# A decoder layer: the recurrence's values and gates projected in pieces of 264, 264 and 512 tokens in place of 264, 264, 256 and 256

## The chip, the core and the metric

The kernel runs on one core of a Trainium2 chip. The metric is the device time of one execution in microseconds (us); the median of several executions is given. The engines are PE (TensorE's matmuls, with PEld its weight loads), DVE (VectorE), ACT (ScalarE), POOL (GpSimd) and SP (SyncE, which here only issues transfers). Each runs its own instructions in order and waits for the others by semaphores. [...]

## The reference

One layer on 16 meta tokens and 1024 tokens of width 1024: a SwiGLU half step, a mixing block of two parallel groups of heads (a gated linear recurrence, HGRN2, with 4 heads of 128, and stick-breaking attention with 8 heads of 64), and a second SwiGLU half step.

```python
h = h + 0.5 * swiglu(rms_norm(h, ffn1_norm[l]), ffn1_w_in[l], ffn1_w_out[l])
u = rms_norm(h, mix_norm[l]) @ w_in[l]
hq, hf, hi, hg, sq, sk, sv = jnp.split(u, ..., axis=-1)
o_hg = hgrn2(hq, hf, hi, hg, lb_all[l], hgrn_out_norm[l], valid)
o_sb = stick_breaking(sq, sk, sv, sb_q_norm[l], sb_k_norm[l], valid)
h = h + jnp.concatenate([o_hg, o_sb], axis=-1) @ w_out[l]
h = h + 0.5 * swiglu(rms_norm(h, ffn2_norm[l]), ffn2_w_in[l], ffn2_w_out[l])
```

In the recurrence, `hf` gives the gate `f = lb + (1 - lb) sigmoid(hf)` and the key `k = (1 - lb) sigmoid(-hf)`, `hi` is the value `v`, `hq` the query and `hg` the gate of the output. Values and keys are needed for all 1040 tokens, queries and output gates for the 1024 behind the meta tokens.

## The kernel before

Activations are kept with the model's width on the partitions and the tokens along the free dimension. Each fp32 operand is split into a high and a low part, and `product` (L250) makes a product from three matmuls per block of 128 rows: high by high (L257), low weights by high (L258), high weights by low (L259). A projected column block (128 columns of `w_in` for n tokens) is therefore 8 x 3 = 24 matmuls of n tokens into one PSUM bank.

The stages, in order of time: the first SwiGLU (to about 690 us in the profile), the attention's projections, then three stages in which the order of PE's instructions is written out by the program:

- **The weave** (`weave`, L1735, over `tasks`, L2164) projects the attention's q, k and v for four pairs of heads (`sb_project`, L1375) while other engines turn and normalise them. At its end it takes the first steps of `hgrn_fill` (L1126): v and f of the recurrence's head 0.
- **The braid** (`braid`, L1705) lays the stick-breaking attention, job by job (score pieces `z`, transposes `flip`, products `oacc`), between further steps of `hgrn_fill`. It sums the planned time of the attention's steps, multiplies it by 1.22, and takes steps of projection from `columns` until that much planned time is covered. What it takes in one round is spread evenly over the round.
- **The rest** (`rest`, L2211) runs the steps of `columns` that are left, while the recurrence's heads (`hgrn_attend`, L1193) load their data back from DRAM and begin; then a second weave runs the recurrence (`lvl`, `km`, `knp`, `s`, `up`, `op`, `onp`) between the steps of the output projection's attention half (`wo`, `mix_out`, L1677). The second SwiGLU follows at about 1325 us.

`hgrn_fill` goes through the heads' columns in the order v, f, q, g. Each column is cut into pieces of tokens: q and g by HALVES (512 and 512), v and f by PIECES. Each piece is two steps of 12 matmuls, and each step carries its planned time, `12 * (n * 0.42 + 13)` ns. Behind the second step of a piece, `use` reads the bank: for v one copy on ACT (L1143), for f two sigmoids on ACT (L1149, L1150) and two operations on DVE (L1151, L1154), for q and g one sigmoid on ACT (L1157) and a product on DVE that reads the bank again (L1158). The results go through buffers `st` to DRAM (`hg_v`, `hg_k`, `hg_f`, `hg_q`, `hg_g`). The tokens from 528 on are written in reverse order, which the recurrence uses.

In the weave the projections take turns between two banks; in the braid one of the two holds a column of zeros for the scans (`idle`), and all pieces use the other (`proj_bank`, L1097, `proj_tags`). The weights of a column are loaded and split ahead of it (`col_tile`, `split_w`: L240 casts the high part on ACT, L242 makes the low part on DVE).

PE's order is the program's. On ACT, DVE, POOL and SP the framework arranges the instructions, so their order can change with PE's.

Of the kernel before, what the change touches and what calls it, by code (L numbers as in the profile page):

```python
# [27 lines left out]
EPS = 1e-6  # L28
HALVES = [(META, 512), (META + 512, 512)]
CHUNKS = [(META + 512, 512), (0, 264), (264, 264)]  # L30
PIECES = [(0, 264), (264, 264), (528, 256), (784, 256)]
LEVELS = [1, 2, 4, 8, 16, 32, 64]
NEG = -1e30

# [15 lines left out]
class Block:  # L50
# [1075 lines left out]
    def hgrn_fill(self, xh, xl, pool, dst):  # L1126
# [56 lines left out]
        for i, (kind, _) in enumerate(plan):  # L1183
            for ci, (c0, n) in enumerate(PIECES if kind in "vf" else HALVES):
                for half in range(2):
# [599 lines left out]
    def run(self):  # L1785
# [21 lines left out]
        with ExitStack() as c0:  # L1807
            with ExitStack() as c1:
# [352 lines left out]
                columns = self.hgrn_fill(xh, xl, pst, hgD)  # L2161
                oH, self.att = [], []

                def tasks():  # L2164
                    done = []
                    for i in range(4):
                        for x in done[i - 2] if i > 1 else ():
                            yield "join", x
                        done.append(
                            (yield from self.sb_project(i, xh, xl, mixb, mix, (qD, kD, vD)))  # L2170
                        )
                        if i == 2:
                            next(jobs)
                    for t, f in islice(columns, 16):
                        f()
                        yield t

                with tc.manual_schedule(engines={nc.tensor.engine}):
                    cf = ExitStack()
                    fetch = self.pool("fetch", ctx=cf, side="right")  # L2180
                    jobs = self.sb_jobs((qD, kD, vD, oD), fetch, self.att)
                    with ExitStack() as c2:
                        mixb = self.pool("mixb", ctx=c2)
                        mix = self.pool("mix", ctx=c2)
                        self.weave(tasks())
                    with ExitStack() as c2:
                        self.att.append(self.pool("att1", ctx=c2))
                        tag = self.proj_tags[0]
                        self.proj_tags = [self.proj_tags[1]] * 2
                        self.idle = self.pproj.tile([P, 1], F32, tag=tag, name="idle", bufs=1)  # L2190
                        nc.vector.memset(self.idle, 0.0)
                        self.braid(jobs, islice(columns, 76), 1.22, 2.0, 3.0)
                    cf.close()
                    self.proj_tags[0] = tag
                    hg_ctx = ExitStack()
                    hg = self.pool("hg", ctx=hg_ctx, side="right")
                    heads = [self.hgrn_attend(h, hg, hgD, oH) for h in range(4)]
                    self.wide = hg.tile([P, 5, 512], U8, name="wide")
                    for i, n in enumerate(LEVELS[:5]):
                        m = self.masks[:, i, :].rearrange("p (b h r) -> p b h r", h=2, r=n)  # L2200
                        wide = self.wide[:, i].rearrange("p (h c x) -> p h c x", h=2, c=4)
                        for half in range(2):
                            for c in range(4):
                                nc.vector.tensor_copy(
                                    wide[:, half, c].rearrange("p (b r) -> p b r", r=n),
                                    m[:, :, 1 - half, :],
                                )
                    for h in range(3):
                        next(heads[h])

                    def rest():  # L2211
                        left = list(columns)
                        for t, f in left[:-1]:
                            f()
                            yield t
                        left[-1][1]()

                    self.weave(rest(), heads[:3], 1e6, 1.0, True)
# [183 lines left out]
```

## Time and profile before

| | us |
|---|---|
| median of 3 runs | 1961.46 |
| lowest, highest | 1961.43, 1961.83 |
| the profiled execution: its time | 1963.76 |
| the profiled execution: its span | 1962.1 |

The profile shows one execution. In a group of instructions stand the line, the engine, the operation, `out<-in` by the names of tiles, and the shapes; then the sum of the busy time, the mean of one in ns, and the engine's idle time ahead of them with what ended it. A timeline row begins with the start in us from the span's begin, then the duration. Matmuls are pipelined: a matmul's duration overlaps with the next one's, so their pace is read from start to start. "SPq" is the issue of a transfer on SP's queue. In the page's slices of the span, PE is at 9 tenths or more everywhere but in the first.

```profile
PE   7999999999999999999999999999999999999999
DVE  6977877877678665467777766667567777767774
ACT  6523443334444544356666635433132332344443
```

### The profile page before, as it was taken

Reading aid. Unit: us, or ns where it says so; the run is one execution under the profiler, and the core shown is the slowest. Engines: PE = TensorE matmul, PEld = TensorE weight load, DVE = VectorE, ACT = ScalarE, POOL = GpSimd, SP = SyncE. Lnnn points to the kernel's source line nnn. Section 1 sums busy time; section 2 is a strip of 40 time slices with the busy share of each in tenths; the row PEclk is TensorE's granted clock in tenths of the full one; section 3 lists DMA queues with packets and bytes.
Section 4 is the critical chain, followed back from the end, with each engine's and each line's share of the span. In section 5 each row is a group of like instructions: output and inputs, shape, how many; then the busy total and the mean of one; then the engine's idle time right before and its main releaser. Section 6 shows DMA issues by size and latency. Waiting matters only on the chain.

```text
span 1962.1 us, 30371 instructions
## 1 busy us (share of the span) xinstructions
PE 1925.3 (98%) x10671; PEld 1616.6 (82%) x10671; DVE 1387.2 (71%) x2185; ACT 849.9 (43%) x1711; POOL 449.7 (23%) x626
## 2 busy tenths in 40 slices
PE   7999999999999999999999999999999999999999
PEld 6888888787888888888888978887888888888887
DVE  6977877877678665467777766667567777767774
ACT  6523443334444544356666635433132332344443
POOL 3010100001000003133333332210544645530000
PEclk9999999999999999999999999999999999999999
DMA  7356887757965415865454178655545444469473
GB/s 212 93 158 177 253 272 241 232 205 284 378 219 188 130 51 144 193 171 148 130 139 127 57 249 221 167 204 183 194 117 145 122 137 119 134 237 328 147 232 113
DMA packets 381687, 355.54 MB, mean 181 GB/s; under 512 B 129040, under 2 KB 284560, under 8 KB 381536
## 3 DMA queue, kind: packets, MB, share of 16 engines
q1 hardware_dynamic: 359728, 288.98, 48.9%
q0 software_dynamic: 20768, 64.63, 9.6%
q8 instruction: 84, 1.38, 0.3%
q14 instruction: 67, 0.55, 0.1%
q10 hardware_dynamic: 1040, 0.00, 0.0%
HBM read 237.95 MB, written 115.57 MB: 180 GB/s over the span
## 4 chain that ended last, share of the span: by engine, by line
PE 88%; DVE 4%; DMA 4%; ACT 1%; issue 1%; SPq 1%; POOL 1%; DVEq 0%; ACTq 0%; POOLq 0%
PE o L740 21%; PE qb L458 18%; PE qa L458 12%; PE qc L458 12%; PE proj L257 4%; PE proj L259 4%; PE proj L258 4%; PE flip L1503 2%; PE wo L258 1%; PE wo L259 1%; PE wo L257 1%; PE mq L1009 1%; PE oacc L1578 1%; PE oacc L1580 1%; PE z L1648 1%
## 5 line engine op out<-in xcount | busy, mean ns | idle before, releaser
L458 PE MATMUL qb<-T,wh 128*128 128x512 f32 x1056 | 344.5, 390 | 1.3 <-ACT T L317 0.8
L458 PEld LDWEIGHTS qb<-T,wh 128*128 128x128 f32 x1056 | 198.1, 188 | 46.3 <-issue 2.5
L458 PE MATMUL qa<-B,wh 128*128 128x512 f32 x696 | 226.7, 390 | 0.1
L257 PE MATMUL proj<-xh,wh 128*128 128x512 f32 (+2 forms) x640 | 213.4, 333 | 2.4 <-ACT st L1150 1.3
L740 PE MATMUL o<-t,w 128*128 128x512 f32 x924 | 212.3, 390 | 0.8 <-DVE u L551 0.7
L259 PE MATMUL proj<-xl,wh 128*128 128x512 f32 (+2 forms) x640 | 209.7, 328 | 0.8 <-DVE xl L1968 0.8
L258 PE MATMUL proj<-xh,wl 128*128 128x512 f32 (+2 forms) x640 | 209.6, 328 | 0.0
L740 PE MATMUL o<-parts 128*128 128x512 f32 x924 | 209.6, 389 | 0.0
L458 PE MATMUL qb<-T,wl 128*128 128x512 f32 x528 | 205.5, 389 | 0.0
L740 PEld LDWEIGHTS o<-t,w 128*128 128x128 f32 x924 | 172.7, 188 | 38.4 <-ACT sgm L989 1.1
L740 PEld LDWEIGHTS o<-parts 128*128 128x128 f32 x924 | 173.5, 188 | 36.0
L370 DVE TENSOR_TENSOR wl<-s,wh 128x512 fp32r<-128x512 f32 x160 | 165.5, 1034 | 51.3 <-ACT wh L368 50.4
L368 ACT CAST wh<-s 128x512 fp32r<-128x512 f32 x160 | 99.3, 622 | 188.7 <-PE qb L458 142.4
L458 PEld LDWEIGHTS qa<-B,wh 128*128 128x128 f32 x696 | 130.5, 188 | 27.6 <-DVE B L844 0.5
L368 ACT CAST wh<-raw 128x512 fp32r<-128x512 f32 x120 | 74.5, 621 | 156.8 <-PE qc L458 111.5
L458 PE MATMUL qa<-B,wl 128*128 128x512 f32 x348 | 135.4, 389 | 0.0
L257 PEld LDWEIGHTS proj<-xh,wh 128*128 128x128 f32 x640 | 120.6, 188 | 14.3 <-ACT st L1150 1.8
L259 PEld LDWEIGHTS proj<-xl,wh 128*128 128x128 f32 x640 | 120.4, 188 | 12.1 <-DVE xl L1968 1.2
L258 PEld LDWEIGHTS proj<-xh,wl 128*128 128x128 f32 x640 | 120.5, 188 | 10.0
L458 PE MATMUL qc<-B,wh 128*128 128x512 f32 x352 | 115.2, 390 | 2.8 <-DVE u L551 2.7
L458 PE MATMUL qc<-T,wh 128*128 128x512 f32 x352 | 117.0, 394 | 0.0
L458 PEld LDWEIGHTS qb<-T,wl 128*128 128x128 f32 x528 | 99.1, 188 | 20.2
(397 smaller groups left out, 3839.0 us busy)
## 6 DMA issues: line engine op xcount, KB each, us to landing
raw<-in_ffn_w_in_dram SPq DMA_DIRECT2D x176, 256.0 KB, 4.0
raw<-in_ffn_w_out_dram SPq DMA_DIRECT2D x112, 256.0 KB, 4.6
w2in<-both SPq DMA_DIRECT2D x28, 512.0 KB, 3.4
raw<-in_w_in_dram SPq DMA_DIRECT2D x25, 512.0 KB, 5.4
ks<-kD SPq DMA_DIRECT2D x32, 260.0 KB, 5.2
wout<-both SPq DMA_DIRECT2D x16, 512.0 KB, 3.7
wh<-w2in SPq DMA_DIRECT2D x27, 256.0 KB, 3.2
wl<-w2in SPq DMA_DIRECT2D x27, 256.0 KB, 3.1
```

What stands on the lines that cost most here:

```text
L257: nc.tensor.matmul(ps, wh[:, s], xs, start=k == 0, stop=False)
L258: nc.tensor.matmul(ps, wl[:, s], xs, start=False, stop=False)
L259: nc.tensor.matmul(ps, wh[:, s], xl[:, k, c0 : c0 + n], start=False, stop=k == nk - 1)
L368: nc.scalar.copy(hi, src)
L370: self.block_lo = nc.vector.tensor_sub(lo, src, hi.bitcast(F32))
L458: nc.tensor.matmul(ps, a[:, k, :], b[:, k, :], start=start and k == 0 and i == 0, stop=k == 3 and i == 2, skip_group_check=True,)
L740: nc.tensor.matmul(banks[bank][m], y[:, m * P : (m + 1) * P], z, start=start and at == 0 and e == 0, stop=q == nq - 1 and e == 2, skip_gro ...
L1009: nc.tensor.matmul(ps[at : at + 32, :], self.xm[:, 4 * h + k, :], got[i, h][:, k, :], start=h == 0 and k == 0, stop=h == 1 and k == 3, til ...
L1503: self.nc.tensor.transpose(ps[:m, j, :], src[:, s0 : s0 + m], self.ident)
L1578: nc.tensor.matmul(o[:, c], vj, w[0], start=j == 0, stop=False, skip_group_check=True)
L1580: nc.tensor.matmul(o[:64, c], vj[:, :64], w[1], start=False, stop=end, skip_group_check=True)
L1648: nc.tensor.matmul(z, q, ks[0][:, s0 : s0 + n], start=True, stop=False)
```

## The change

PIECES becomes three pieces, with one of 512 tokens where two of 256 were. A v or f column is then 6 steps and not 8, a head's four columns are 20 and not 24; the numbers of steps that the first weave and the braid may take at most follow from that, so that head 0's v and f stay in the weave and head 3's g stays behind the braid.

```diff
-PIECES = [(0, 264), (264, 264), (528, 256), (784, 256)]
+PIECES = [(0, 264), (264, 264), (528, 512)]
...
-                    for t, f in islice(columns, 16):
+                    for t, f in islice(columns, 12):
...
-                        self.braid(jobs, islice(columns, 76), 1.22, 2.0, 3.0)
+                        self.braid(jobs, islice(columns, 64), 1.22, 2.0, 3.0)
```

On PE 192 rows disappear (7048 before, 6856 now). A step of 512 tokens has a planned time of 2736 ns, one of 256 has 1446, so the braid now reaches its covered sum with other steps in each round.

On ACT, at the start of the braid, the rows of the difference, from the last evictions of head 0's f on (L1149, L1150), over the first scores' activations (L1654, L1655), to the cast of a weight column (L240):

```order
 L1150 ACTIVATE st<-proj 128x264
-L1149 ACTIVATE st<-proj 128x256
-L1150 ACTIVATE st<-proj 128x256
-L240 CAST wh<-raw 128x1024
-L1149 ACTIVATE st<-proj 128x256
-L1150 ACTIVATE st<-proj 128x256
 L1654 ACTIVATE keep<-z 128x144
 L1655 ACTIVATE sig<-z 128x144
+L1149 ACTIVATE st<-proj 128x512
+L1150 ACTIVATE st<-proj 128x512
+L1654 ACTIVATE keep<-z 128x272
+L240 CAST wh<-raw 128x1024
```

The cast stood ahead of the last f eviction and of every score; now it stands behind the first two pieces of the scores' `keep`, and so does the one eviction of 512 stand behind the first of them.

On PE, at the end of the braid, where the attention's last products (`oacc`) stand, before:

```order
L1578 MATMUL oacc<-wu,v 128x256
L1580 MATMUL oacc<-wu,v 64x256
L1578 MATMUL oacc<-wu,v 128x128
L1580 MATMUL oacc<-wu,v 64x128
L1578 MATMUL oacc<-wm_7895,v 128x256
L1580 MATMUL oacc<-wm_7896,v 64x256
L257 MATMUL proj<-xh,wh 128x512
```

and with the change, at the same place:

```order
L258 MATMUL proj<-xh,wl 128x512
L259 MATMUL proj<-xl,wh 128x512
L1578 MATMUL oacc<-wu,v 128x256
L1580 MATMUL oacc<-wu,v 64x256
L1578 MATMUL oacc<-wu,v 128x128
L1580 MATMUL oacc<-wu,v 64x128
L1578 MATMUL oacc<-wm_7895,v 128x256
L1580 MATMUL oacc<-wm_7896,v 64x256
L257 MATMUL proj<-xh,wh 128x512
```

A step of 12 matmuls (the first half of the second piece of head 3's q) has moved from behind the last products to ahead of their last six; behind the braid stand 5 steps of projection instead of 6.

On PE behind the braid, from the end of the fifth of those steps to the recurrence's first levels (`lvl`; `flip<-vT` turns the values of a head), before:

```order
L259 MATMUL proj<-xl,wh 128x512
L1243 MATMUL lvl<-QA,KB 128x128 x8
L1503 MATMUL flip<-ident,vT 16x128
L1503 MATMUL flip<-ident,vT 128x128 x8
L257 MATMUL proj<-xh,wh 128x512
```

and with the change:

```order
L259 MATMUL proj<-xl,wh 128x512
L1243 MATMUL lvl<-QA,KB 128x128 x8
L1503 MATMUL flip<-ident,vT 16x128
L1503 MATMUL flip<-ident,vT 128x128 x8
L1503 MATMUL flip<-ident,vT 16x128
L1503 MATMUL flip<-ident,vT 128x128 x8
L1278 MATMUL lvl<-QA,KP 128x2x64 x4
L1243 MATMUL lvl<-QA,KB 128x128 x8
L257 MATMUL wo<-oT,wh 128x512
```

The last step of projection between the second head's values and the third's is gone (it was the sixth), and the first `wo` step follows behind one `lvl` of KP, where before it followed behind three. At the end of this weave 6 matmuls of `wo`, where 12 were, stand between the recurrence's last products (`op`) and its last transposes (`onp`).

## The prediction

> **What bounds the kernel now.** The page comes first: shares of the engines, then the chain that ended last.
>
> ```profile
> span 1962.1 us, 30371 instructions
> PE 1925.3 (98%) x10671; PEld 1616.6 (82%) x10671; DVE 1387.2 (71%) x2185; ACT 849.9 (43%) x1711; POOL 449.7 (23%) x626
> PE 88%; DVE 4%; DMA 4%; ACT 1%; issue 1%; SPq 1%; POOL 1%; DVEq 0%; ACTq 0%; POOLq 0%
> ```
>
> PE is busy 98% of the span and holds 88% of the chain. So time goes only where PE has less to do or waits less, and comes only where it waits more. Next come the windows of the stretch in which the projections run. The first is the head of `hgrn_fill` in the weave (v and f of head 0); the others, in turn, are the q and g columns of a head (pieces of 512) and the v and f columns of the next (264, 264, 256, 256), braided with the attention; the last is the rest of the braid.
>
> ```profile
> 836.50:861.00 24.50, 23.21 (x193) 23.00 (x192) 14.18 (x24) 13.70 (x28) 8.58 (x15) 1.00 0.58 171
> 861.00:908.40 47.40, 45.21 (x266) 36.61 (x266) 34.95 (x55) 31.27 (x79) 17.63 (x26) 1.00 0.61 156
> 908.40:954.40 46.00, 45.13 (x373) 42.94 (x372) 36.44 (x60) 32.96 (x88) 18.58 (x28) 1.00 0.52 153
> 954.40:995.50 41.10, 40.19 (x240) 33.46 (x239) 26.62 (x42) 23.22 (x58) 12.10 (x19) 1.00 0.52 137
> 995.50:1040.60 45.10, 44.85 (x368) 42.52 (x367) 35.31 (x59) 32.52 (x88) 16.91 (x23) 1.00 0.44 126
> 1040.60:1083.80 43.20, 41.27 (x250) 34.48 (x248) 29.95 (x50) 26.97 (x70) 15.91 (x25) 1.00 0.44 128
> 1083.80:1129.50 45.70, 44.96 (x371) 42.78 (x371) 32.06 (x54) 29.54 (x76) 15.26 (x18) 1.00 0.15 51
> 1129.50:1139.30 9.80, 9.53 (x59) 7.98 (x57) 4.37 (x10) 4.13 (x10) 0.87 (x2) 1.00 0.23 80
> sum 302.80, PE 294.35 PEld 263.76 DVE 213.87 ACT 194.32 POOL 105.84; mean PE 36.79 PEld 32.97 DVE 26.73 ACT 24.29 POOL 13.23
> ```
>
> After each stretch come its length and the busy time of PE, PEld, DVE, ACT and POOL. PE is idle for 302.80 - 294.35 = 8.45 us in all: no gain in waits can be larger there. The granted clock is 1.00 throughout.
>
> **The change, part by part.** The sum is made against the profiled execution's own 1963.76 us (span 1962.1 and 1.7 around it), which lies 2.3 us above the median 1961.46; those 2.3 are taken off at the end.
>
> *Pace of the matmuls.* Eight columns (v and f of four heads) lose 24 matmuls each: 192 pairs of 256 become 192 single ones of 512.
>
> ```profile
> 842.34 0.28 PE L257 MATMUL proj<-xh,wh 128*128 128x256 f32 x1
> 848.01 0.29 PE L257 MATMUL proj<-xh,wh 128*128 128x264 f32 x1
> 1139.28 0.40 PE L257 MATMUL proj<-xh,wh 128*128 128x512 f32 x1
> 1150.40 1.30 PE L1503 MATMUL flip<-ident,vT 128*16 128x128 f32 x9
> ```
>
> The first and second row enclose 48 matmuls of 256: 5.67 / 48 = 0.1181 us from start to start. The third and fourth enclose 48 of 512: 11.12 / 48 = 0.2317. A pair costs 0.2362, a single one 4.5 ns less: 192 x 4.5 ns = **-0.9 us**. The durations shown (0.28, 0.40) overlap and are not the price. [...]
>
> *Fewer changes of work on PE.* In the braid twelve steps of 12 matmuls fall away.
>
> ```profile
> 861.28 0.48 PE L257 MATMUL proj<-xh,wh 128*128 128x512 f32 x1
> 861.59 0.39 PE L258 MATMUL proj<-xh,wl 128*128 128x512 f32 x1
> ```
>
> Here a step's first matmul, behind a bf16 one, takes 0.31 us to the next start, 0.08 over the pace; at 1139.28 nothing like it is seen. Twelve times 0 to 0.08, so 0 to -1.0: **-0.5**.
>
> *The bank.* In the braid all projections share one bank, and a piece waits until ACT, or DVE, has read the one before it.
>
> ```profile
> 1083.84 0.39 PE L257 MATMUL proj<-xh,wh 128*128 128x264 f32 x1 [0.66 <-DVE st L1158]
> 1139.11 0.33 PE L1580 MATMUL oacc<-wm,v 128*64 128x256 f32 x1 [0.27 <-DVE wm L1627]
> L1157 ACT ACTIVATE st<-proj 128x512 f32<-128x512 f32 x16 | 9.6, 598 | 29.9 <-PE proj L259 29.9
> ```
>
> The first row is the only such wait on PE in the braid: head 3's first v piece behind g. In the new order 44 other matmuls stand between the two, before 29, so it goes: **-0.7**. A larger piece is read longer: an f of 512 by two activations like q's in the third row, 0.6 us each. But behind every one of them 37 to 47 other matmuls stand before the next piece, which cover the 1.2 us; without that cover it would be exposed in three f columns, +3.6. The second row lies in the last attention products of the braid. A projection step now stands in front of them and gives DVE 2.8 us more, so the wait goes: **-0.3**.
>
> *ACT at the start of the braid.* The order shows that the cast of a weight column (L240) now stands behind the first score's activations, not ahead of them.
>
> ```profile
> 862.23 1.05 ACT L240 CAST wh<-raw 128x1024 fp32r<-128x1024 f32 x1 [3.15 <-DMA raw<-in_w_in_dram]
> 864.66 0.40 ACT L1654 ACTIVATE keep<-z 128x272 f32<-128x272 f32 x1 [0.47 <-PE z L1651]
> 865.00:869.00 4.00, 3.12 (x14) 1.72 (x13) 3.75 (x7) 4.00 (x12) 1.50 (x5) 1.00 0.64 177
> ```
>
> Before, it ran while PE did a q step. From 865 to 869 ACT is full (4.00 of 4.00) and PE waits for it (3.12 of 4.00). The cast now falls into that stretch, behind which the score pieces queue on ACT and PE waits for their banks: between 0 (had it room) and +1.05; **+1.0**.
>
> *Coarser cover.* The steps of projection stand between transposes that wait for ACT and DVE. The stretches of 512 from 954.4 and 1040.6 leave PE idle 2.84 of 84.3 us, 3.4%; those of small pieces 1.86 of 136.8, 1.4%. Half of the small ones' work becomes 512: 2.0% of half of 136.8 is +1.4, of all of it +2.8; that the idle of small pieces vanishes would be -1.9. The difference may come from q's and g's own evictions, so half of +1.4: **+0.7**. Up to here -0.9 - 0.5 - 0.7 - 0.3 + 1.0 + 0.7 = **-0.7 us**.
>
> *The hand-over behind the braid.* A half of head 3's q, 12 x 0.2317 = 2.8 us, moves from behind the braid's last attention products to before them. PE's work stays the same, but the loads of the recurrence wait for the end of the attention.
>
> ```profile
> 1142.48 0.37 SPq L1207 DMA_DIRECT2D vT<-hg_v  x1
> 1146.69 7.58 DMA KB<-hg_k
> 1154.28 9.13 DMA F<-hg_f
> 1164.74 6.69 DMA oT<-oD
> 1171.47 0.50 PE L257 MATMUL wo<-oT,wh 128*128 128x512 f32 x1 [1.45 <-DMA oT<-oD]
> 1160.98 0.32 SPq L230 DMA_DIRECT2D wh<-wout  x1
> 1150.00:1154.00 4.00, 4.00 (x23) 3.19 (x22) 0.97 (x2) 1.77 (x4) 2.06 (x4) 1.00 1.05 417
> 1183.68 1.05 PE L1278 MATMUL lvl<-QA,KP 128*128 128x128 f32 x8
> 1184.49 0.48 PE L257 MATMUL wo<-oT,wh 128*128 128x512 f32 x1
> ```
>
> The chain goes from the braid's end through SP's queue and the loads to the third step of `wo`, 32.2 us behind 1139.28, with the DMA engines full (1.05, 417 GB/s): that distance is data, not PE. The braid now ends 2.8 - 0.7 = 2.1 us later, and the whole of it moves along: 24 loads of three heads, the two of `wout` and eight of `oT` on SP. One thing gets shorter: the load at 1160.98 waited for the last projection, which now ends earlier (between 0 and -1.2; -0.6). When the third step of `wo` starts, PE has by the new order also done one group of `lvl` less (the last two rows, 0.8 us from start to start). So PE is then 2.1 - 0.6 + 0.8 = **+2.3 us** behind where it was. The ends: were the loads no limit, PE would stand at the braid's -0.7; with a braid that gains nothing it would stand at 2.8 + 0.8 = +3.6. I take the chain, since PE waited 1.45 us at its end already.
>
> *The end of the weave.* Before the recurrence's last transposes stand 6 matmuls of `wo` now, 12 before.
>
> ```profile
> 1277.39 0.38 PE L1362 MATMUL onp<-ident,vT 128*128 128x128 f32 x2
> 1276.96 0.69 DVE L1356 TENSOR_TENSOR vT<-op,ss 128x512 f32<-128x512 f32 x1
> ```
>
> PE would come 6 x 0.232 = 1.4 earlier, at 1276.0, finish four transposes of the first half by 1276.4, and wait for DVE's end at 1277.65: **+1.2** (0 to 1.4). Waits of PE for DVE in between may shrink while PE is late (0 to -1.3, the bound being DVE's and DMA's other short waits there): **-0.4**.
>
> The sum: +2.3 + 1.2 - 0.4 = +3.1 (the braid's -0.7 is inside the first). 1963.76 + 3.1 - 2.3 = **1964.5 us**. The steps of the stages before 836 and behind 1325 are the same.
>
> **The rivals.** *Slower*: the larger pieces win nothing in the braid, because its waits grow as fast as the pace gains, and the hand-over then costs its whole 2.8 + 0.8 = 3.6; with the 1.2 at the end and a cover at +1.4 in place of +0.7 that is about +5.5: 1967. It decides once the braid ends more than 2.7 us late, since then the sum is over 3.9. For it: the chain through the loads and a full DMA. Against it: 8.45 us of idle leave room for gains. *The hand-over is free*: SP's loads overlap better than the chain says, or PE finds work; what is left is -0.7 and part of +1.2: 1961.5. *Faster*: the braid's waits mostly go, some 4 of the 8.45 us, with the 0.9 and 0.5 and no loss behind: about -5, 1956.5. Against it: ACT's and DVE's orders are both dense in the braid.
>
> *Weight loads*: were the 256s held up by their loads, each would save the difference.
>
> ```profile
> L257 PEld LDWEIGHTS proj<-xh,wh 128*128 128x128 f32 x640 | 120.6, 188 | 14.3 <-ACT st L1150 1.8
> ```
>
> 192 x (188 - 118) ns = 13.4 us, 1948. But a 256 starts every 118 ns under loads shown as 188, so loads are hidden. [...] That the change does not do what it says is out: PE has 192 rows fewer.
>
> **How the numbers follow.** Forecast 45%, slower 30%, hand-over free 15%, faster 9%, weight loads 1%. What a measurement can tell from no change is about 0.2%, 3.9 us: 1957.5 to 1965.4. The forecast's own range, 1962 to 1967, reaches past the upper end: some 6 of its 45 go there, so slower 36%, same 54%, faster 10%. The range: the braid's terms at their low ends (-0.9 - 1.0 - 0.7 - 0.3 + 0 - 1.9 = -4.8) the braid ends 2.0 early, PE stands at -2.0 - 1.2 + 0.8 = -2.4 behind the loads, and with -0.4 and no loss at the end at -2.8: 1959. At their high ends (-0.9 + 1.0 + 2.8 = +2.9) the braid ends 5.7 late, and 0.8 and the end's 1.2 make +7.7: 1969.
>
> **What would show it.** Right: 512s from start to start at 0.232 in v and f; an idle PE of 4 to 6 us ahead of the third `wo` step, released by the load of `oT`; the last transposes waiting for L1356; the L240 cast inside the first scores. Wrong: the idle of the braid's windows below 5 or above 11 us, or a `wo` that starts without waiting.

## The result, and the profile after

| | before | after |
|---|---|---|
| median, us | 1961.45 (6 runs) | 1975.46 (6 runs) |
| lowest, highest | 1959.79, 1961.94 | 1973.67, 1977.60 |
| profiled execution: time, span | 1963.76, 1962.1 | 1977.31, 1975.6 |

The ratio is 1.0071 (95% interval 1.0061 to 1.0081): 14.0 us slower, outside the predicted range of 1959 to 1969, where +3.1 was forecast.

The page of the change, its span, PE's row and the chain's shares by engine:

```profile
span 1975.6 us, 29932 instructions
PE 1928.5 (98%) x10479; PEld 1609.9 (81%) x10479; DVE 1390.3 (70%) x2177; ACT 847.3 (43%) x1699; POOL 449.9 (23%) x626
PE 88%; DVE 6%; ACT 2%; DMA 2%; issue 2%; POOL 1%; SPq 0%; DVEq 0%; ACTq 0%; POOLq 0%
```

The 192 matmuls are gone (10671 to 10479), and the shares of the page hardly move. DVE's and ACT's part of the chain is up: 6 and 2% against 4 and 1%. The starts of the same work on PE, from both timelines, say where the time went:

| PE starts, us | before | after | difference |
|---|---|---|---|
| first scores of the braid | 861.06 | 860.65 | -0.4 |
| v of head 1 | 908.46 | 909.20 | +0.7 |
| v of head 2 | 995.56 | 997.71 | +2.2 |
| v of head 3 | 1083.84 | 1088.57 | +4.7 |
| last output product of the braid | 1139.11 | 1150.01 | +10.9 |
| first `wo` on `oH`, behind the weave | 1278.18 | 1291.86 | +13.7 |

Of the 10.9 at the braid's end 2.8 are the q half that moved there. So the braid lost 10.9 + 0.4 - 2.8 = 8.5 us, and the weave behind it 13.7 - 8.1 = 5.6. Nothing is lost outside.

The windows of the change, for the head of the projections in the weave, for the four stretches that begin with the first scores and with the v of a head, up to the braid's end (columns as in the prediction):

```profile
836.10:860.60 24.50, 23.06 (x145) 20.76 (x144) 13.42 (x22) 12.89 (x25) 8.57 (x15) 1.00 0.56 165
860.60:909.20 48.60, 45.29 (x265) 36.63 (x265) 35.65 (x55) 31.85 (x79) 18.42 (x26) 1.00 0.59 155
909.20:997.70 88.50, 85.23 (x564) 73.84 (x563) 62.90 (x99) 55.55 (x143) 31.13 (x45) 1.00 0.49 140
997.70:1088.60 90.90, 86.72 (x562) 75.26 (x561) 63.86 (x101) 56.20 (x144) 31.37 (x46) 0.98 0.43 122
1088.60:1150.20 61.60, 57.84 (x399) 51.21 (x398) 39.24 (x66) 35.11 (x90) 17.69 (x23) 1.00 0.18 61
sum 314.10, PE 298.14 PEld 257.69 DVE 215.07 ACT 191.60 POOL 107.18; mean PE 59.63 PEld 51.54 DVE 43.02 ACT 38.32 POOL 21.44
```

PE's idle time is 314.10 - 298.14 = 16.0 us, before 8.45, and in the fourth row the granted clock (the number behind POOL's) is 0.98. What PE waited for in the braid, before (in all, how often, the longest):

```profile
PE flip L1503 <- DVE wu L1627: 2.7, 6, 0.7
PE flip L1503 <- DVE wm L1627: 1.5, 3, 0.6
PE z L1648 <- ACT sig L1655: 1.1, 4, 0.5
PE proj L257 <- DVE st L1158: 0.7, 1, 0.7
PE oacc L1580 <- DVE wm L1627: 0.3, 1, 0.3
```

and with the change:

```profile
PE flip L1503 <- DVE wu L1627: 6.2, 12, 1.0
PE flip L1557 <- DVE wu L1627: 3.1, 3, 1.5
PE z L1648 <- ACT sig L1655: 2.8, 5, 1.2
PE flip L1503 <- DVE wm L1627: 1.8, 4, 0.5
PE oacc L1580 <- DVE wu L1627: 0.2, 1, 0.2
```

The transposes (`flip`) of the attention's weights waited 4.2 us and now wait 11.1. A `flip` tile lies in one of two banks (the two buffers of the kernel's pool `ptr` in PSUM, the memory of the tiles that PE writes here); it is free once ACT has cast it (L1626) and DVE has taken the rest (L1627). So the wait for `wu` or `wm` is that of a tile for the tile before the last. PE's timeline with the change shows one:

```profile
1020.15 0.60 PE L1503 MATMUL flip<-ident,sig 128*128 128x128 f32 x4
...
1022.82 0.39 PE L1557 MATMUL flip<-ident,sig 128*16 128x128 f32 x2 [1.47 <-DVE wu L1627]
...
1024.37 0.88 PE L1503 MATMUL flip<-ident,sig 128*128 128x128 f32 x3 [0.69 <-DVE wu L1627]
1024.89 0.57 PE L257 MATMUL proj<-xh,wh 128*128 128x264 f32 x1
1025.26 0.42 PE L258 MATMUL proj<-xh,wl 128*128 128x264 f32 x1
...
1027.02 0.42 PE L257 MATMUL proj<-xh,wh 128*128 128x264 f32 x1
```

Three groups of transposes lie close together, with no projection step among them. Behind them the matmuls of 264 start 0.22 us apart, where their pace is 0.12: the granted clock is 0.51 in the second of these windows of the change, and 1.00 in the first.

```profile
1020.50:1023.90 3.40, 1.72 (x13) 1.11 (x11) 3.40 (x4) 2.66 (x7) 0.68 (x2) 1.00 0.49 151
1023.90:1027.30 3.40, 2.93 (x14) 2.96 (x15) 2.53 (x5) 0.48 (x1) 1.40 (x1) 0.51 0.67 140
```

That is an estimated 1.4 us more (13 matmuls from 1024.37 to 1027.24 take 2.87 us; at full pace three transposes of 0.09, as from 1020.15 to 1020.50, and ten of 0.12 take 1.5). The braid's loss is then named: transposes +6.9, scores +1.7, half clock +1.4, the bank wait gone -0.7, `oacc` -0.1, pace of 144 matmuls in the braid -0.65: +8.5. All of this is read from one execution of each kernel.

### The profile page after: what moved, and what is told of

It is laid out like the page before. It is cut to its first block, busy times and chain, and to the rows that moved or that the text cites. A ratio compares the mean times of both kernels' runs of the same rounds, so it can differ in the third digit from the quotient of the medians.

```text
span 1975.6 us, 29932 instructions
## 1 busy us (share of the span) xinstructions
PE 1928.5 (98%) x10479; PEld 1609.9 (81%) x10479; DVE 1390.3 (70%) x2177; ACT 847.3 (43%) x1699; POOL 449.9 (23%) x626
## 4 chain that ended last, share of the span: by engine, by line
PE 88%; DVE 6%; ACT 2%; DMA 2%; issue 2%; POOL 1%; SPq 0%; DVEq 0%; ACTq 0%; POOLq 0%
PE o L740 21%; PE qb L458 18%; PE qa L458 12%; PE qc L458 12%; PE proj L257 4%; PE proj L259 4%; PE proj L258 4%; PE flip L1503 1%; PE wo L258 1%; PE wo L259 1%; PE wo L257 1%; PE mq L1009 1%; PE oacc L1578 1%; PE oacc L1580 1%; DVE keep L1658 1%
## 5 line engine op out<-in xcount | busy, mean ns | idle before, releaser
L257 PE MATMUL proj<-xh,wh 128*128 128x512 f32 (+1 forms) x576 | 202.3, 351 | 3.2 <-ACT st L1150 1.4
L259 PE MATMUL proj<-xl,wh 128*128 128x512 f32 (+1 forms) x576 | 199.5, 346 | 0.8 <-DVE xl L1968 0.8
L258 PE MATMUL proj<-xh,wl 128*128 128x512 f32 (+1 forms) x576 | 199.5, 346 | 0.0
L257 PEld LDWEIGHTS proj<-xh,wh 128*128 128x128 f32 x576 | 109.0, 189 | 16.9 <-DVE st L1158 1.8
L259 PEld LDWEIGHTS proj<-xl,wh 128*128 128x128 f32 x576 | 108.8, 189 | 14.8 <-DVE xl L1968 1.2
L258 PEld LDWEIGHTS proj<-xh,wl 128*128 128x128 f32 x576 | 109.0, 189 | 12.1
L1664 POOL TENSOR_TENSOR sig<-sig,keep 128x144 f32<-128x144 f32 (+3 forms) x64 | 81.7, 1277 | 158.9 <-DVE keep L1658 86.5
```

Source lines behind the costliest of these rows:

```text
L257: nc.tensor.matmul(ps, wh[:, s], xs, start=k == 0, stop=False)
L258: nc.tensor.matmul(ps, wl[:, s], xs, start=False, stop=False)
L259: nc.tensor.matmul(ps, wh[:, s], xl[:, k, c0 : c0 + n], start=False, stop=k == nk - 1)
L1664: nc.gpsimd.tensor_mul(sig, sig, keep[:, 1 : nk + 1])
```

## The experiments

**Theory**: the order of the work in the braid loses the time. Twice as long steps of projection come half as often, so more often none lies between transposes, and the step that moved to the braid's end is missed behind it. **Rivals**: the larger bank and its eviction lose it; the first head's pieces do; DVE and ACT are late by themselves. Each ratio is to the kernel before in runs beside it, with its 95% interval.

| run | us | ratio, interval |
|---|---|---|
| e1: order of before, one bank and eviction of 512 | 1961.52 | 0.9998 (0.9988 to 1.0007) |
| e2: pieces of before, order of the change | 1973.49 | 1.0065 (1.0050 to 1.0080) |
| e3: the change, its 512s of v and f in 4 steps of 6 | 1969.26 | 1.0041 (1.0026 to 1.0056) |
| e5: the change, q half left behind the braid | 1969.81 | 1.0043 (1.0028 to 1.0058) |
| e6: e3 and e5 together | 1962.08 | 1.0006 (0.9997 to 1.0015) |
| e9: 512s for the first head alone | 1963.84 | 1.0014 (1.0005 to 1.0023) |
| e12: e6, first head as before | 1961.37 | 0.9999 (0.9990 to 1.0008) |
| e7: all 512s, q and g too, in steps of 6 | 1997.01 | 1.0178 (1.0164 to 1.0191) |
| e8: before, q and g in steps of 6 | 1996.74 | 1.0185 (1.0170 to 1.0199) |
| e10: e7, behind the braid by two | 1962.17 | 1.0003 (0.9994 to 1.0012) |
| e11: e8, behind the braid by two | 1961.76 | 0.9999 (0.9990 to 1.0008) |
| e13: the change, third bank for transposes | 1968.79 | 1.0034 (1.0021 to 1.0046) |
| e14: before, third bank | 1956.22 | 0.9972 (0.9961 to 0.9984) |
| e15: e12, third bank | 1956.41 | 0.9970 (0.9959 to 0.9981) |
| e16: before, tile of zeros in SBUF | 1967.16 | 1.0024 (1.0014 to 1.0033) |
| e17: before, third bank shared with the zeros | 2065.43 | 1.0529 (1.0515 to 1.0543) |
| e18: e12, third bank shared with the zeros | 2078.92 | 1.0602 (1.0587 to 1.0616) |

**Pieces or order (e1, e2).** e1 keeps PE's order of before, with two 256s side by side in one bank of 512 and one eviction; e2 keeps the pieces of 256 and their evictions, and makes each one step.

In e1, for such a piece (four steps of 12):

```
+                cc = 256 * (half // 2)
+                self.product(
+                    kept["ps"][:, cc : cc + 256], kept["w"], xh, xl, c0 + cc, 256,
+                    range(4 * (half % 2), 4 * (half % 2) + 4),
+                )
```

In e2, with the limits 12 and 64 of the change:

```
+            ks = range(8) if half is None else range(4 * half, 4 * half + 4)
...
-                for half in range(2):
+                for half in [None] if n == 256 else range(2):
```

> One bank and one eviction of 512 tokens as in the change, but the 512 are computed as two halves of 256 in the steps of before: PE's order is that of before. Theory 1 (the order on PE costs: steps of 2.8 us leave the attention's transposes without cover): within 2 us of before, 1959.5 to 1963.5, and PE's waits for DVE wu as before, about 2.7 us in the braid. Theory 2 (the wider evictions cost, because ACT and DVE are held longer in one piece): near the change, 1971 to 1977, with waits for wu of about 6 us.

> Pieces and evictions of 256 as before, but each 256 piece is one step of 24 matmuls (2.83 us), so that PE's order of steps is that of the change. Theory 1 (order on PE): near the change, 1972 to 1978 (0.9 us more than it for the pace), with waits for wu above 5 us in the braid. Theory 2 (wider evictions): near before, 1960 to 1964.

e1 is not to be told from the kernel before; e2 loses most of the change's loss without one 512-token matmul in v or f. PE's waits for `wu` in the braid of e1:

```profile
PE flip L1517 <- DVE wu L1641: 2.5, 5, 0.7
```

and of e2:

```profile
PE flip L1503 <- DVE wu L1627: 4.9, 10, 1.0
PE flip L1557 <- DVE wu L1627: 1.7, 2, 1.0
```

With those for `wm` the transposes wait 3.4 us in e1 and 8.4 in e2. So in the order of before the bank and the eviction are free, and the order alone loses time. Where it loses it differs: in e2's profile (1976.75 us, the slowest of its four runs) the braid without the moved half loses 4.4 us (282.5 against 278.1), and the weave behind it 9.1, with two half clock windows (from 1170.4 and 1201.1; the mean granted clock of this execution is 0.998); the change loses 8.5 and 5.6. The scores wait 1.6 in e2 and 2.8 in the change, and e2's braid has no half clock. So in the order of the change the wide pieces may still cost some 4 us in the braid; that is not separated here, and the runs of the two overlap (1972.8 to 1976.8 and 1973.7 to 1977.6).

**Steps in the braid, and the step behind it (e3, e5, e6).**

In e3, the number of steps of a piece (limits 16 and 76; in e6 16 and 74):

```
+        def parts(i, n):
+            return 4 if n == 512 and plan[i][0] in "vf" else 2
```

In e5, against the change:

```
-                        self.braid(jobs, islice(columns, 64), 1.22, 2.0, 3.0)
+                        self.braid(jobs, islice(columns, 62), 1.22, 2.0, 3.0)
```

> The change's 512 pieces, each in four steps of 6 matmuls (1.4 us) instead of two of 12, so steps are as long as those of before. Theory 1: back to before and 1 to 2 us below it for pace and bank, 1959 to 1963. Theory 2: stays near the change, 1971 to 1977.

> The change, with the braid's limit at 62 steps, so that the half of head 3's q stands behind the attention's last products again, as before. Theory of the hand-over (the loads wait for the braid's end, 2.8 us each way): 2 to 3.5 us below the change, 1971.5 to 1973.5. If the hand-over costs nothing because all after the braid is later anyway: within 1 us of the change, 1974.5 to 1976.5.

> The run with the v and f 512-token pieces in four steps of 6 matmuls (1969.3), but with the last q half left behind the braid as in the kernel before. If the two losses add up (cover inside the braid, and the order at the braid's end, which gave 5.6 us when put right in the change itself), the time is 1963 to 1965. If the 5.6 us belonged to something that the finer steps had already mended, it stays at 1968 to 1970.

The step left behind the braid is worth 1975.46 - 1969.81 = 5.6 us, which is what the table of starts had put there. e3 alone misses its forecast by 6 us, since it mends only the braid; e5 lies 1.7 below its own. The profiles divide it so: without the moved half the braid takes 278.9 us in e3 (278.1 before), but 286.7 in e5 (286.6 in the change), and from the braid's last product to the first `wo` on `oH` e5 takes 138.5 (139.1 before). From e5 to e6 the finer steps give 7.7, and with both the loss is gone: 1962.08, 1 to 3 us less than the sum of the two had promised, and still with every 512-token piece. The waits of the change behind the braid show what was missed:

```profile
PE flip L1503 <- DVE vm L1228: 2.4, 2, 2.0
PE knp L1314 <- DVE kms L1308: 1.9, 4, 0.6
PE onp L1362 <- DVE vT L1356: 1.7, 1, 1.7
PE proj L257 <- DVE st L1158: 1.4, 1, 1.4
```

The first is the same two banks again. The timelines of DVE and PE with the change:

```profile
1172.38 1.41 DVE L1265 TENSOR_TENSOR KB<-KB,Ts 128x512 f32<-128x512 f32 x1 [0.81 <-ACT KP L1272]
1173.71 0.27 DVE L1228 COPY vm<-flip 16x128 f32<-16x128 f32 x1
...
1174.04 1.03 PE L1503 MATMUL flip<-ident,vT 128*128 128x128 f32 x4 [2.03 <-DVE vm L1228]
```

The third head's values are turned right behind the second's, since the projection step between them is gone. Their bank is released by a copy that stands behind a product on DVE, which waited for ACT. Behind it the clock is halved a second time (below).

**The first head (e9, e12).**

In e9 `PIECES` is that of before, and `WIDE` (264, 264, 512) serves the first head (with the weave's limit at 12); in e12 the other way round, with `NARROW` (264, 264, 256, 256).

```
-            for ci, (c0, n) in enumerate(PIECES if kind in "vf" else HALVES):
+            for ci, (c0, n) in enumerate(HALVES if kind in "qg" else PIECES if i > 1 else WIDE):
```

> 512-token pieces for the v and f of the first head only, whose projections run beside the output projection ahead of the braid; all steps in the braid and behind it are those of the kernel before. Theory (only the braid and what follows it lose): pace 48 x 4.5 ns = -0.2 us and what the last cast of the piece does to the first scores, at most +1; time 1960.5 to 1962.5, no difference that can be measured. Rival (a 512-token piece loses outside the braid too, by its bank that is held twice as long): 1963 or more.

> The run at 1962.1 (v and f pieces of 512 in four steps of 6, the last q half behind the braid), but with the first head's v and f in the pieces of before (256 and 256). If the +2.3 of the run with 512-token pieces in the first head alone is the cast of that piece ahead of the first scores, it goes: 1959.5 to 1961, equal to or just below the kernel before. If that loss lies elsewhere (or was the clock of that run), it stays at 1961.5 to 1963.

e9 is 2.3 us slower, 0.14%: 1.3 us above what the theory allowed, and within the rival's "1963 or more". In its profile the scores wait 2.1 us (before 1.1), and its granted clock was 0.998 or 0.999 in seven of eleven runs, where the kernel before had 1.000 in 20 of 21. Taken out again in e12 the first head's wide pieces give 0.7, inside both intervals, and 1961.37 falls between the two ranges that were expected. Their price in the change lies between nothing and 2.3, and was not settled.

**Every step short (e7, e8, e10, e11).** Here q and g go in steps of 6 as well, so that, by a count, no transposes are left without cover: I add up PE's work, at the paces of the prediction, between the end of a group of transposes and the start of the next but one. Of 126 such gaps 10 are under 2.0 us in the kernel before, 19 in the change, 12 in e3, e6 and e12, none in these four. (In e1 there are 10 and in e2 19, as in the kernels whose order they keep.) e10 and e11 differ from e7 and e8 only behind the braid:

```
-  for t, f in left[:-1]:
+  for (t, f), (_, g) in zip(left[:-2:2], left[1:-2:2]):
       f()
+      g()
-      yield t
+      yield 2 * t
```

> All three pieces of a v or f as in the change (264, 264, 512), but every 512-token piece, those of q and g too, goes into the braid in four steps of 6 matmuls, and 72 matmuls are left behind the braid as in the kernel before. Theory 1 (a transpose tile waits for one of its two banks, which is free only once the cast and the DVE have used the tile before the last, and the length of the projection steps between them decides whether that shows): in the order, no two transpose tiles two apart have less than 2.0 us of matmuls between them (10 of 126 have in the kernel before, 19 in the change), so TensorE's waits for wu of 4.2 us before and 9.3 in the change go to under 1; with the pace of the 512-token matmuls (-0.9) and the bank wait that goes (-0.7) the time is 1956 to 1959, below both kernels. Theory 2 (512-token pieces cost by themselves, by their bank or their casts): the time stays above the kernel before, 1964 to 1975. Theory 3 (which waits fall where is luck of the order): anywhere from 1960 to 1970, with waits for wu of 4 us or more.

> The kernel before with its pieces of 264, 264, 256 and 256; only its q and g steps of 12 matmuls on 512 tokens are cut into steps of 6 in the braid, with 72 matmuls left behind it as before. Theory 1 (length of the steps): here too no gap between transposes is under 2.0 us in the order, so the 4 us of waits for wu go, and the time is 1957 to 1959.5; against the run with all 512-token pieces in steps of 6 it lacks the pace and the bank wait, some 1 to 1.5 us. Theory 2 (the 512-token v and f pieces cost by themselves): this one is 4 us or more below the run with 512-token pieces in steps of 6. Theory 3 (luck): 1960 to 1965.

> As the run with all 512-token pieces in four steps of 6 matmuls, but the steps behind the braid are taken two at a time, so that the order behind the braid is that of the kernel before word for word. In the run without this, the braid took 278.8 us (first score 860.79 to last output matmul 1139.56; the kernel before 278.1), and 35 us were lost behind it, where twelve single steps let the head streams run 135 lvl matmuls without a wo step beside them. If that is all, the time is 1959.5 to 1962.5: the waits of the transposes (10.8 us in the change's braid for wu and wm, 1.6 here) are gone, and in their place stand waits of a piece's first matmul for its one bank (5.0 us against 0.7). If the shorter steps lose by themselves, the time stays at 1970 or above.

> The kernel before with its q and g steps cut into steps of 6 in the braid, taken two at a time behind it. Its braid took 277.5 us in the run without the pairs (860.23 to 1137.75; the kernel before 278.1). Expected 1960 to 1962: the transposes' waits go from 4.2 to some 2.4 us and the bank waits come up from 0.7 to 3.9. A gain over the kernel before of more than 0.1% would speak for the length of the steps alone; a time of 1970 or above for a loss of its own in the order behind the braid.

The forecast of a gain failed twice. e7 and e8 lose 35 us behind the braid: by its code the weave gives a head its turn whenever one is ready, and takes a step only otherwise; with twelve short steps 135 `lvl` matmuls ran before the next step came. The window of e7 shows PE busy 20.20 of 28, DVE 28.00, a clock of 0.82 and DMA engines that move hardly anything (a share of 0.02):

```profile
1162.00:1190.00 28.00, 20.20 (x129) 18.32 (x128) 28.00 (x43) 9.92 (x19) 10.08 (x21) 0.82 0.02 5
```

With the steps taken by two (e10, e11) that is mended, but the time only equals that of the kernel before. The waits of e10 in the braid say why:

```profile
PE proj L257 <- DVE st L1158: 3.7, 8, 0.7
PE flip L1508 <- DVE wu L1632: 1.5, 3, 0.7
PE proj L257 <- ACT st L1150: 1.3, 2, 0.8
```

The transposes wait 1.5 us in place of 4.2, and the pieces wait 5.0 in place of 0.7 for the one bank that all projections of the braid share. One wait took the place of the other. Nor does the count alone give the wait: with no gap under 2.0 us the transposes still wait 1.5 us in e10 and 2.4 in e11; with 10 gaps 3.4 in e1 and 4.2 before, with 12 some 6.7 in e3, e6 and e12, with 19 8.4 in e2 and 11.1 in the change.

**The number of banks (e13 to e18).** The braid leaves one projection bank to `idle`, one column of zeros that DVE's scan reads. e13, e14 and e15 move it to SBUF and give the bank to every third tile of transposes, in an unchanged order; e16 moves the zeros alone.

```
+    def turn_bank(self, shape):
+        self.turns += 1
+        if self.third and self.turns % 3 == 0:
+            return self.pproj.tile(shape, F32, tag=self.third, name="flip", bufs=1)
+        return self.ptr.tile(shape, F32, tag="tr", name="flip")
...
-  self.idle = self.pproj.tile([P, 1], F32, tag=tag, name="idle", bufs=1)
+  self.idle = self.att[-1].tile([P, 1], F32, name="idle")
```

> The change with nothing else altered in TensorE's order, but the transposes of the braid go round three PSUM banks instead of two: the third is the projection bank that the braid leaves to a one-column tile of zeros (idle), which moves to SBUF. Theory 1 (the transposes wait for the bank of the tile before the last, because the long projection steps leave too little work between them): the transposes' waits of 11.1 us in the change's braid for wu and wm go to under 2, the half-clock window near 1024 us goes with them, and the braid takes 8 to 10 us less; the loss in the order at the braid's end (5.6) stays, so 1966 to 1968. Theory 2 (the cast and the DVE that follow the transposes are late by themselves; the bank only names where it shows): the same waits turn up at the output matmuls (oacc) or the scores (z), and the time falls by less than 3 us, 1972.5 or above.

> The kernel before with three banks for the transposes in the same way. Theory 1: its 4.2 us of waits for wu and wm go, 1957.5 to 1959. Theory 2: 1961 to 1962. If reading the zeros from SBUF slows the scan, this run and the control both rise.

> The run at 1961.4 (v and f pieces of 512 tokens in four steps of 6 from the second head on, the first head in 256s, the last q half behind the braid) with three banks for the transposes. Theory 1: its waits for wu and wm in the braid, 6.7 us, go, 1955.5 to 1958, below both kernels; if the bank is no limit any more, nothing but the pace of the 512-token matmuls (144 x 4.5 ns = 0.65) and one bank wait stands between it and the kernel before with three banks. Theory 2: 1960 to 1962.

> Control: the kernel before with the one-column tile of zeros in SBUF, the transposes on their two banks as before. If the scan reads the zeros as fast from there, 1961 to 1962.5, no difference; if it is slower, the scan's rows are longer and the time may rise, by at most what the first scores wait for.

PE's waits of e13 from 858 to 1150 us; of the first row 1.4 lie behind the braid's end, where the change has the same wait:

```profile
PE proj L257 <- DVE st L1158: 2.9, 3, 1.4
PE z L1654 <- ACT sig L1661: 2.8, 5, 1.2
PE oacc L1586 <- DVE wu L1633: 2.7, 4, 1.1
PE flip L1509 <- DVE wu L1633: 1.0, 3, 0.5
```

and of e14 in the same stretch:

```profile
PE z L1654 <- ACT sig L1661: 1.1, 4, 0.5
PE proj L257 <- DVE st L1158: 0.9, 2, 0.7
...
```

With the order kept, the third bank takes the transposes' waits from 11.1 to 1.0 us in the change and from 4.2 to none in the kernel before. So the bank is the limit, though DVE's scans have become slower (in the control, e16, 1132 ns on average, 875 before): the control loses 5.0 us. That loss fits the same cause, banks that come free later behind slower scans: in e16, in the order of before, the transposes wait 9.3 us in place of 4.2, and the braid takes 283.0 in place of 278.1. Counted against the control, the third bank is worth 1967.16 - 1956.22 = 10.9 us to the kernel before, and e14 lies 1.3 us below what was forecast for it. But theory 2 holds a part. In e13 2.7 us turn up at `oacc` and 1.5 at the projections' bank in the braid, the clock is halved once near 868 in place of 1024 (0.99 in the mean from 860.5 to 1142.0), the braid gains 8.3 (289.4 to 281.1 us from first score to last product), and the whole only 6.7, so that its time lies 0.8 above what theory 1 allowed. e13 stays 12.6 above e14. If the braid's end costs the 5.6 of e5 here too, the long steps still lose about 7; in the profiles the braid of e13 without the moved half is 5.3 us longer (278.3 against 273.0), with waits of 8.0 us in all against 3.4. e14 and e15 are faster than both kernels (1956.2 and 1956.4), and equal: once the transposes have their bank, the 512-token pieces, in short steps, bring nothing that can be measured.

e17 and e18 kept the zeros in the last column of that third bank and put the transposes of up to three tiles beside them.

```
+  self.third = self.pproj.tile([P, 512], F32, tag=tag, name="third", bufs=1)
+  self.idle = self.third[:, 511:512]
```

> The kernel before, in which the transposes of one to three tiles and the 16-row ones use the bank of the one-column tile of zeros as their third bank, and the zeros stay in that bank's last column (those of four tiles keep the two banks). In the run with the zeros in SBUF the scan took 1124 ns in place of 875 (112 scans, 28 us of the DVE more), and the control lost 5.0 us by it. If the scan is back at 875 and the transposes' waits stay away, the time is below the three-bank run (1956.2): 1951 to 1955. If the shared bank makes transposes and scans wait for each other, or four-tile transposes still wait for their two banks, it is 1957 or above.

> The same third bank for the version with v and f pieces of 512 tokens in four steps of 6 from the second head on (1956.4 with the zeros in SBUF): 1951 to 1955 by the first reading, 1957 or above by the second. Between this run and the one on the kernel before, 512-token pieces are worth at most the pace, 0.65 us, and a bank wait of 0.7.

They lose 104 and 117 us. PE's waits in e17:

```profile
PE third L1562 <- DVE keep L1663: 42.5, 21, 3.6
PE third L1508 <- DVE keep L1663: 21.0, 13, 3.1
```

Transposes wait for scans that only read the zeros in the same tile. So it is open what a third bank would give with the zeros left in PSUM but in another bank.

## Why the prediction was wrong

- **The step that failed is "coarser cover", +0.7 with ends at -1.9 and +2.8.** This was the term for thinner work between the transposes. It measured +6.9 of waits of the transposes and +1.4 of half clock, for which the prediction had no term: 8.3 in all. I had taken the idle share of the stretches with 512-token steps (3.4%) over that of the small ones (1.4%), as if idle time grew with the share of large steps. It does not: a group of transposes waits when too little work stands since the last but one, and of such gaps there are 19 where 10 were. The order, which was at hand, would have given the count, though not the time; the two rows of averages could give neither. e3 shows the cause from one side (the same pieces in short steps bring the braid back to within 0.8 us), e13 and e14 from the other (a third bank takes the waits away). How much of the 8.3 the order alone causes, and how much the wide pieces in that order, stays open (e2: 4.4 in the braid).
- **Hand-over.** Predicted: 2.3 - (-0.7) = 3.0 lost between the braid's end and the third `wo` step, then -0.4 and 1.2 at the weave's end, 3.8 in all. Measured: 5.6, by the starts and by e5. The third `wo` step starts at 1181.98 and not at 1171.47, 10.5 later; with the 0.8 of `lvl` that is still to do and without the braid's 8.5, 2.8 are lost up to there. That this is near 3.0 is luck: the step waited for no `oT`, so the chain of loads did not hold it. In its place PE waited for the transposes' bank (`vm`, 2.4 new) and the projections' bank (1.4 new) and lost an estimated 1.7 in a half clock window, while the waits for `oT` and for the load of `vT` are gone. Behind that step 2.8 are lost where 0.8 were forecast. In all, the waits behind the braid went from 6.6 to 9.5 us; with the half clock 4.6 of the 5.6 are named.
- **End of the weave.** Predicted +1.2 by DVE's L1356 ahead of `onp`; the wait is there with 1.7 us, for the cause that was named.
- **ACT's cast** at the braid's start. Predicted +1.0; the scores wait 1.7 us more, and the rows of ACT and PE with the change show the cast where the order had it:

```profile
864.54 1.04 ACT L240 CAST wh<-raw 128x1024 fp32r<-128x1024 f32 x1
...
865.93 0.47 PE L1648 MATMUL z<-ks,qs 128*128 128x456 f32 x1 [1.18 <-ACT sig L1655]
```

- **Pace.** Right by the rows: with the change twelve matmuls of 512 in head 0's pieces, from 844.29 to 847.07, start 0.232 us apart. Up to the first score PE is 0.4 us ahead, of which the 48 matmuls of the first head give 0.2. The -0.5 for fewer changes of work was not seen apart; the braid's sum comes out without it.
- **The bank wait** at head 3's v went as predicted (0.7 before, none in the braid with the change); the tail's 0.3 for `wm` went too, and 0.2 for `wu` took its place. One of 1.4 us came up at the bank behind the braid.
- **Rivals.** "Slower" was the right sign and the right pair of causes (waits of the braid, whole hand-over) at two fifths of the size. Both signs of being wrong that the prediction names came: the braid's windows have 16.0 us of idle, over 11, and the third `wo` step started without waiting. That weight loads hide a gain of 13.4 us is out: e15, with the wide pieces in three heads, is no faster (1956.41 us) than e14 without them (1956.22).

## What to carry to other kernels

Where filler work stands between producers that share a ring of few buffers, the length of a filler step is a schedule decision of its own: count, in the order, the work between each use of a buffer and its next, and compare that with the time of its release, before larger tiles are tried. The count says where waits are to be feared; in e10 and e11 it did not say how long they are. A finer step is not free either: it brings the next piece sooner to its own bank (e10), and a planner that counts time by steps may run dry (e7). If the waits name a ring, one more buffer is the direct test, and here it beat both kernels (1956.2 and 1956.4 us), while the tile size, in short steps, made no difference that could be measured.

## What the runs showed of the hardware

**The granted clock fell behind short stalls.** In the change PE's granted clock is 1.00 up to 1023.9 and 0.51 for the next 3.4 us; in the 3.4 us ahead of the fall PE was still busy for 1.72, and its longest wait was 1.47. It falls a second time, in these windows of the change:

```profile
1170.60:1174.00 3.40, 1.01 (x6) 0.51 (x5) 2.58 (x5) 1.74 (x3) 3.07 (x7) 1.00 1.06 389
1174.00:1177.40 3.40, 3.36 (x16) 3.36 (x17) 0.59 (x1) 1.13 (x2) 2.55 (x13) 0.52 1.03 321
```

In windows of 0.1 us the clock is 0.50 from 1024.0 to 1027.3 and from 1174.2 to 1177.5, and 1.00 again from 1027.4 and from 1177.6: both low stretches last 3.4 us. PE was not idle ahead of them: in the 3.40 us up to each fall (from 1020.59 and 1170.75) it was busy for 1.62 and 1.04, about half of one and a third of the other (there with transposes alone). In the kernel before the least busy 3.40 us between 860 and 1200 have 1.95 of PE, and the clock stayed at 1.00:

```profile
1170.00:1173.40 3.40, 1.95 (x13) 1.55 (x13) 3.40 (x6) 0.62 (x1) 0.41 (x3) 1.00 0.99 366
```

The mean granted clock of the profiled execution was 0.998 in the change and in e2, 0.999 in e3 and e5 and 0.997 in e13, against 1.000 before. Taken with the falls, the two stalls of the change, with longest waits of 1.47 and 2.03 us, cost more than their length: an estimated 1.4 us (above) and 1.7 (half of the second 3.4).

**With the zeros in SBUF the scans took longer where GpSimd's multiplication ran beside them.** Rows of DVE in the braid, with the zeros in PSUM (before) and in SBUF (e16); beside the first GpSimd's L1664 runs from 943.00 for 1.13 us, beside the second from 945.28 for 1.12:

```profile
943.30 0.84 DVE L1658 TENSOR_TENSOR_SCAN keep<-keep,idle 128x329 f32<-128x329 f32 x1
```

```profile
945.59 1.51 DVE L1658 TENSOR_TENSOR_SCAN keep<-keep,idle 128x329 f32<-128x329 f32 x1
```

The 112 scans take 126.8 us in e16 and 98.0 in the kernel before (14 shapes, 8 of each, by their means). In e16, 45 of them run beside GpSimd's multiplication (L1664) and take 28.9 us more in all than the shortest of their size in either kernel; 57 run beside nothing on GpSimd and take 0.7 more. In the kernel before, 46 run beside it and take 0.6 more. What makes them longer was not shown: no run tried it by itself.
